# Hybrid encoder step on one core: pool weights folded into the output projection, roots by DRAM, chunk pairs in two column groups, large tiles at multiples of 256 bytes

## The chip, the cores and the metric

The kernel runs on one core of one Trainium2 chip. The metric is the device time of one execution in microseconds (us). A kernel is timed several times and the median counts; beside that, one execution is recorded by the hardware profiler, and its instructions, waits and DMAs make the profile that is read here.

A core has TensorE (PE: matrix products into PSUM), VectorE (DVE), ScalarE (ACT), GpSimd (POOL), and SyncE (SP), which here only issues DMAs.

## The reference, cut to what matters

One layer of a streaming encoder, for a prompt of 2,048 frames and for 32 further frames of a running stream (the sample), with the same weights. All is float32.

```python
h = rmsnorm(x, g_pre_mix)                      # (frames, 1024)
z = h @ w_in                                   # 1024 -> 2560: u | q | f | i | g, 512 each
# mixer A: four groups of 128 channels, windows 2, 4, 8, 16
d = (windowed_sum(u) / count - u)              # per group, trailing window
y_pool = einsum('blgc,gcd->blgd', d, w_pool) * pool_scale
# mixer B: gated linear recurrence, 4 heads x 128, exact, in chunks
o = hgrn(silu(q), (1 - lb) * sigmoid(-f), i, log(lb + (1 - lb) * sigmoid(f)))
y_hg = rmsnorm(o, g_hg_norm) * silu(g)
x = x + rmsnorm(concat(y_pool, y_hg) @ w_out, g_post_mix)
h2 = rmsnorm(x, g_pre_ffn)
x = x + rmsnorm((silu(h2 @ w_gate) * (h2 @ w_up)) @ w_down, g_post_ffn)
```

The outputs are x for prompt and sample, the last 15 rows of u, and the recurrence's final state, for each of the two.

## The kernel before

The prompt is worked in two halves of 1,024 frames, A and B; the 32 sample frames ride along with B. For each half come, in order: the value projection (`vps`), four heads (three projections each into `mmb`, and beside them the recurrence), the four pool groups (one projection each, then window and pool weights), the output projection (`project`, into `ops`), and the gate and up projections (`gate_up`, into `gx`, `gy`, `gz`, `gw`, by a Strassen-like scheme of seven products). After both halves comes the down projection (`down`, into `dx`, `dy`, `dz`).

Each float32 operand of a large product is split into a high and a low part of type float32r, and a product is three matmuls, high x high, high x low and low x high, each of 128 x 128 by 128 x 512 (`mm`, line 179). A half takes 192 of them for the values, 768 for the heads and pool groups, 384 in `project` and 1,848 in `gate_up`; `down` takes 1,848; together 2 x 3,192 + 1,848 = 8,232. The smaller products (recurrence, sums, pool weights, sample) are plain float32; the trace shows each of these as two records.

**What sets the order.** PE's order is the order in which the code emits its instructions. A clock counted in the code (`Pace.t`) adds the cost of every matmul; beside the main stream there are tasks (`Task`: the recurrence of a head, the pool products of a group, the second norm, the statistics of half B), generators that yield a delay. `poll()` runs a task's next step once the clock has passed it, so PE's small products stand among the large ones at chosen distances. `finish()` runs a task to its end on the spot. The orders of the other engines and of the DMA queue of SP are made by a scheduler from what each instruction needs.

**Memory.** Large tiles (`ztile`, `xtile`, lines 90 to 94) come from the pool UP with 39 slots of `TMAX` = 1,056 floats, 4,224 bytes, which is 16.5 x 256: in the built program the slots begin, by turns, at a multiple of 256 bytes and 128 bytes past one. The tiles of 512 floats (`t2`, pool TP, 22 slots of 2,048 bytes) all begin at multiples of 256. Of the operands of large products, `hThi`, `hTlo`, `yhi`, `ylo`, `fhi`, `flo`, `wf`, `dhi`, `dlo` and `whw`, `wlw` lie in UP; `whi`, `wlo` and most of `hst` lie in TP.

**The places that the change touches.**

- Pool groups (`pool_products`, `pool_window`, `pool_mix`, lines 916 to 983): ACT copies a group's projection into `e_t`; DVE makes the trailing window by one to four shifted sums between `sa` and `sb` and a last step that subtracts, emitted in one piece behind the group's projection; later, as a task, PE multiplies by the pool weights `wpool` into `pps` (two float32 products of 128 x 512 for each group and half), and ACT and DVE split the result into `yhi` and `ylo`. In half B the sample's 32 frames go the same way, and two transposes for each group (`nps`) turn the last 15 rows for the outputs.
- `late_constants` (line 153) loads `wpool` and the sample's pool history and transposes the latter (`cps`).
- Roots: the norm of a half multiplies each frame by its reciprocal root. For half B, `later_stats` (line 437) makes the roots as a column for each 128 frames; POOL lays them on a diagonal (`dg`, line 482), and PE multiplies with a matrix of ones to have them along the rows (`rb`, line 457). The sample is normalised by rows and transposed (`stps`, line 369).
- Recurrence (`hgrn`, line 722): 1,024 frames are 8 chunks of 128. Within a chunk, pairwise products are made level by level: `group` (line 736) for blocks of 32 frames, each product 32 columns wide (`gb`, four column groups in turn); then the level of pairs of 32 (line 805, into `gb`, column groups 0 and 2), and the level of 64 (line 811, into `lv`, 64 columns wide, always PSUM rows 0 to 63). ACT copies these last two into `attn` (lines 818 and 819). DVE carries the state from chunk to chunk (`S`, line 873), and the products `ops` read `attn` and `S`. `f_t`, `k_t`, `q_t`, `qa` are a head's gates and keys, `tt` their running products, `kd` the turned keys, `ups` the state's increments, `on` the head's normalised output.

Of the kernel before, what the change touches and what calls it, by code (L numbers as in the profile page):

```python
# [16 lines left out]
P = 128  # L17
D = 1024
# [11 lines left out]
NT = 22  # L30
# [4 lines left out]
TMAX = HALF + NS  # L35
CHUNK = 128
# [41 lines left out]
def body(tc, ins, outs, cst):  # L78
    nc = tc.nc
    ctx = ExitStack()  # L80
    with ctx:
# [7 lines left out]

        def ztile(name, shape=None, dt=F32):  # L90
            return UP.tile(shape or [P, TMAX], dt, tag="u", name=name)

        def xtile(name, shape=None):
            return UP.tile(shape or [P, TMAX], F32R, tag="u", name=name)
# [46 lines left out]
        wpool = CP.tile([P, 4, P], F32, name="wpool")  # L141
        hist = CP.tile([P, 4, 16], F32, name="hist")
        shist = CP.tile([P, 4, 16], F32, name="shist")
# [9 lines left out]
        def late_constants():  # L153
            nc.sync.dma_start(out=wpool, in_=ins["w_pool"][0].rearrange("g c d -> c g d"))
            cachet = ztile("cachet", [HIST, 512])
            nc.sync.dma_start(out=cachet, in_=ins["cache_pool"][0, 0])
            cps = axbank("cps")
            for g in range(4):
                nc.tensor.transpose(cps[:, 16 * g:16 * g + HIST], cachet[:, g * P:(g + 1) * P], ident[0:HIST, 0:HIST])
            nc.vector.tensor_copy(shist[:, :, 0:HIST], cps[:, 0:64].rearrange("p (g t) -> p g t", g=4)[:, :, 0:HIST])  # L160
# [276 lines left out]
        def later_stats(S):  # L437

            st = S.st
            for i in range(NCH):  # L440
                for c in range(2):
                    x = t2("xtl")
                    r0 = S.tok0 + i * P
                    nc.sync.dma_start(out=x, in_=x_p[r0:r0 + P, c * 512:c * 512 + 512])
                    sumsq(x, P, st[:, 2 * i + c:2 * i + c + 1])
                    del x
                yield 20000.0
            ev = st[:, 0:16].rearrange("p (i c) -> p i c", c=2)
# [3 lines left out]
            S.rs = [[st[:, 24 + 4 * tg + i:25 + 4 * tg + i] for i in range(4)] for tg in range(2)]  # L452
# [22 lines left out]
        def front_norm(S, tg):  # L475
            if tg == 0:
                S.hsr = SP.tile([P, KD, NS], F32, tag="hs", name="hsr", bufs=1)
                S.ysr = SP.tile([P, KD, NS], F32, tag="ysr", name="ysr", bufs=1)
            channel_tiles(S, tg)
            S.dg[tg] = t2("dg", [P, 4, P])  # L480
            for i in range(4):
                nc.gpsimd.tensor_scalar(S.dg[tg][:, i], ident, S.rs[tg][i], None, ALU.mult)
            if tg == 1:
                xq = ztile("xts", [NS, D])
                nc.sync.dma_start(out=xq, in_=x_s)
# [3 lines left out]
            if tg == 1:  # L489
                st = new_stat()  # L490
                sumsq(xq, NS, st[0:NS, 0:1])
                nc.vector.tensor_scalar(xq, xq, rstd_of(st, NS), None, ALU.mult)
            yield from scaled_channels(S, tg)
            if tg == 1:
                sample_to_channels(xq, g_pre, S.hsr)


        def front_loads(S):
# [223 lines left out]
        def hgrn(S, H, h):  # L722
# [9 lines left out]
            blks = [(c, j, gb[c // 4][32 * j:32 * j + 32, (c % 4) * 96:(c % 4 + 1) * 96]) for c in range(NCH) for j in range(4)]  # L732
            if B:
                blks.append((NCH, 0, gb[1][32:64, 384:480]))

            def group(goff, src, pick, n=16):
                join()
                for c, j, out in blks:
                    c0 = c * P + 32 * j
                    mm(out[:, goff:goff + n], k_t[:, c0:c0 + 32], pick(src[:, c0:c0 + 32]), True, True, 36.0)  # L740
# [21 lines left out]
            def masked(dst, bank, row0, col0, nch, r):  # L762
                bv = bank[row0:row0 + r, col0:col0 + 96 * nch].rearrange("p (c x) -> p c x", x=96)
                for i in range(NGRP):
                    mk = cons[row0:row0 + r, C_MASK + 16 * i:C_MASK + 16 * i + 16].bitcast(I32).unsqueeze(1).broadcast_to([r, nch, 16])
                    src = bv[:, :, 16 * i:16 * i + 16]
                    if i == 1 or i == 2:
                        src = bv[:, :, 16:48].rearrange("p c (b y) -> p c b y", y=4)[:, :, :, 2 * i - 2:2 * i]
# [32 lines left out]
            for c in range(NCH):  # L801
                o = 384 + (c % 4) * 32
                for j in (0, 2):
                    c0 = c * P + 32 * j
                    mm(gb[c // 4][32 * j:32 * j + 32, o:o + 32], k_t[:, c0:c0 + 32], qa[:, c0 + 32:c0 + 64], True, True, 55.0)
# [4 lines left out]
            for c in range(NCH):  # L810
                mm(lv[0:64, c * 64:c * 64 + 64], k_t[:, c * P:c * P + 64], qa[:, c * P + 64:c * P + 128], True, True, 112.0)
            yield 0.0
            t7 = merge(6, tc_)
            for sb in range(2):
                masked(cmp_[sb], gb[sb], 0, 0, 4, P)
                bv = gb[sb][:, 384:512].rearrange("p (c x) -> p c x", x=32)
                for j in (0, 2):
                    nc.scalar.copy(attn[sb][32 * j:32 * j + 32, :, 32 * j + 32:32 * j + 64], bv[32 * j:32 * j + 32])
                nc.scalar.copy(attn[sb][0:64, :, 64:128], lv[0:64, sb * 256:sb * 256 + 256].rearrange("p (c x) -> p c x", x=64))
                if B and sb == 1:  # L820
                    masked(cmps, gb[1], 32, 384, 1, 32)
# [94 lines left out]
        def pool_products(S, g):  # L916
            e_t = ztile("e_t")
            es = small("es", [P, 48], bufs=2) if S.B else None
            nc.vector.tensor_copy(e_t[:, 0:HIST], hist[:, g, 0:HIST])
            w = take()  # L920
# [7 lines left out]
            S.pools[g] = S.pool = Task(pool_mix(S, g, e_t, es), (9000.0 if S.B else 14000.0) if g > 1 else (7000.0 if S.B else 9000.0), after=S.pool)  # L928
            pool_window(S, g, e_t, es)

        def pool_window(S, g, e_t, es):
            w = WINDOWS[g]

            def window(src, L, bufs, d, first):
# [8 lines left out]
                nc.vector.scalar_tensor_tensor(d[:, 0:L], cur[:, HIST:n], 1.0 / w, src[:, HIST:n], ALU.mult, ALU.subtract)  # L943
# [5 lines left out]
            S.d[g] = sb if w in (2, 8) else sa  # L949
            window(e_t, HALF, (sa, sb), S.d[g], not S.B)  # L950
            if not S.B:
                nc.vector.tensor_copy(hist[:, g, 0:HIST], e_t[:, HALF:HALF + HIST])
            else:
                nc.vector.tensor_copy(es[:, 0:HIST], shist[:, g, 0:HIST])
                s1, s2 = small("es1", [P, 48], bufs=2), small("es2", [P, 48], bufs=2)
                S.ds[g] = s2 if w in (2, 8) else s1
                window(es, NS, (s1, s2), S.ds[g], False)

        def pool_mix(S, g, e_t, es):
            S.y[g] = (ztile("yhi", dt=F32R), ztile("ylo", dt=F32R))  # L960
            d_t = S.d[g]
            for sbk in range(2):
                ps = axbank("pps")
                mm(ps, wpool[:, g, :], d_t[:, sbk * 512:(sbk + 1) * 512], True, True, 858.0)
                hi, lo = S.y[g]
                cols = slice(sbk * 512, (sbk + 1) * 512)
                nc.scalar.activation(hi[:, cols], ps, AF.Copy, scale=p_scale[:, g:g + 1])
                nc.vector.scalar_tensor_tensor(lo[:, cols], ps, p_scale[:, g:g + 1], hi[:, cols].bitcast(F32),
                                               ALU.mult, ALU.subtract)
# [736 lines left out]
```

## Time and profile before

| | |
|---|---|
| Time, median of 3 runs | 2145.66 us (2145.22 to 2146.64) |
| The profiled execution's own time | 2145.8 us |
| Its span, first to last instruction | 2144.0 us |
| PE busy | 2124.1 us (99%), 13,176 matmul records |
| DVE, ACT, POOL busy | 1431.6, 822.0, 281.6 us |
| DMA | 316.19 MB, mean 147 GB/s |
| Granted TensorE clock, mean | 0.998 |

The stages in the profiled execution, roughly: values of half A to 52 us, its heads and pool groups to 292, its output projection to 362, gate and up to 795; half B the same from there to 1,690; the down projection to 2,136; the last rows to 2,144.

How to read the rows that the prediction shows: a group's row gives line, engine, operation, output <- inputs and shape, then busy time and mean duration of one in ns, then idle time ahead of it with what ended it. A matmul's record lasts longer than the distance to the next one, since matmuls overlap in the array; what a matmul costs is read from the distance between starts, or from the time that a stretch takes divided by its matmuls. A timeline row gives the start, the duration in us, and how many records were merged. A window's row gives its length, the busy time with the number of records, the granted clock, the DMA engines' busy share and the rate.

### The profile page before, as it was taken

To read this page: it belongs to the slowest core of one execution; us is meant where nothing else is said; L and a number is where in the kernel's file an instruction comes from. 1 tells how busy PE (TensorE), PEld (TensorE's weight loads), DVE (VectorE), ACT (ScalarE), POOL (GpSimd) and SP (SyncE) were. 2 spreads that over 40 slices of the span, in tenths; PEclk is the share of its full clock that TensorE was granted. 3 is DMA by queue.
4 is the path that set the end of the run, shared out by engine and by line. 5 is a ranking of instruction groups with operands and counts; after the bars stand their busy time and mean duration, and the time that the engine had idled before them with its cause. 6 is when DMAs were issued, how large, how long until landed. Compare 5 with 4: busy or idle time off the path is not lost.

```text
span 2144.0 us, 34134 instructions
## 1 busy us (share of the span) xinstructions
PE 2124.1 (99%) x13176; PEld 1702.8 (79%) x13176; DVE 1431.6 (67%) x2330; ACT 822.0 (38%) x1605; POOL 281.6 (13%) x382
## 2 busy tenths in 40 slices
PE   9999999999999999999999999999999999999998
PEld 8788778888888887788867778888888777877876
DVE  6655665787776778355574697767667756466487
ACT  6434335544444445233323664444444521011032
POOL 1223301100000010122320220000000211110134
PEclk9999999999999999999999999999999999999999
DMA  8121134445545559011004624544445796776778
GB/s 305 50 70 56 35 128 157 128 123 167 157 144 156 148 162 286 27 44 34 25 23 149 189 85 131 156 143 143 144 143 145 234 323 197 224 222 189 223 214 217
DMA packets 388783, 316.19 MB, mean 147 GB/s; under 512 B 16007, under 2 KB 318335, under 8 KB 388622
## 3 DMA queue, kind: packets, MB, share of 16 engines
q1 hardware_dynamic: 386174, 306.11, 46.5%
q0 software_dynamic: 2016, 7.34, 1.8%
q8 instruction: 104, 1.70, 0.3%
q14 instruction: 57, 0.47, 0.1%
q10 hardware_dynamic: 432, 0.57, 0.1%
HBM read 215.60 MB, written 98.37 MB: 146 GB/s over the span
## 4 chain that ended last, share of the span: by engine, by line
PE 82%; DVE 4%; ACT 1%; issue 1%; POOL 1%; DMA 1%; DVEq 0%; POOLq 0%; SPq 0%; ACTq 0%
PE gx L180 21%; PE gy L180 11%; PE dx L180 10%; PE mmb L180 10%; PE ops L180 9%; PE dy L180 5%; PE gz L180 4%; PE dz L180 3%; PE vps L180 2%; PE gw L180 1%; PE gsps L180 1%; PE gb L180 1%; DVE acc L1493 1%; PE ups L180 1%; PE pps L180 1%
## 5 line engine op out<-in xcount | busy, mean ns | idle before, releaser
L180 PE MATMUL gx<-fhi,wf 128*128 128x512 f32 x1376 | 449.1, 395 | 0.0
L180 PEld LDWEIGHTS gx<-fhi,wf 128*128 128x128 f32 x1376 | 258.3, 188 | 61.4 <-issue 2.2
L180 PE MATMUL gx<-flo,wf 128*128 128x512 f32 x688 | 270.0, 392 | 0.0
L180 PE MATMUL gy<-fhi,wf 128*128 128x512 f32 x704 | 233.0, 393 | 0.1
L180 PE MATMUL mmb<-hThi,whi 128*128 128x512 f32 x512 | 217.6, 425 | 0.0
L180 PE MATMUL dx<-dhi,hst 128*128 128x512 f32 x640 | 213.4, 394 | 0.5 <-DVE acc L1493 0.4
L180 PE MATMUL mmb<-hThi,wlo 128*128 128x512 f32 x512 | 201.7, 394 | 0.0
L180 PE MATMUL mmb<-hTlo,whi 128*128 128x512 f32 x512 | 201.5, 394 | 0.0
L1493 DVE TENSOR_TENSOR acc<-dx,acc 128x512 f32<-128x512 f32 x168 | 115.2, 689 | 75.9 <-PE dx L180 75.2
L1217 DVE TENSOR_TENSOR wf<-s,wf 128x512 fp32r<-128x512 f32 x176 | 120.1, 689 | 62.2 <-ACT wf L1212 59.6
L180 PEld LDWEIGHTS gy<-fhi,wf 128*128 128x128 f32 x704 | 132.2, 188 | 31.2 <-DVE c L1315 0.5
L180 PEld LDWEIGHTS gx<-flo,wf 128*128 128x128 f32 x688 | 129.4, 188 | 28.3
L1212 ACT CAST wf<-s 128x512 fp32r<-128x512 f32 x176 | 108.3, 621 | 101.0 <-PE gy L180 30.3
L180 PEld LDWEIGHTS dx<-dhi,hst 128*128 128x128 f32 x640 | 120.1, 188 | 32.2 <-issue 3.4
L180 PE MATMUL gy<-flo,wf 128*128 128x512 f32 x352 | 138.2, 393 | 0.0
L180 PE MATMUL dx<-dlo,hst 128*128 128x512 f32 x320 | 125.5, 392 | 0.0
L1217 DVE TENSOR_TENSOR wf<-wraw,wf 128x512 fp32r<-128x512 f32 x132 | 89.8, 688 | 44.2 <-ACT wf L1212 44.1
L180 PEld LDWEIGHTS mmb<-hThi,whi 128*128 128x128 f32 x512 | 96.6, 189 | 24.4 <-issue 5.4
L180 PEld LDWEIGHTS mmb<-hThi,wlo 128*128 128x128 f32 x512 | 96.4, 188 | 22.3
L180 PE MATMUL dy<-dhi,hst 128*128 128x512 f32 x320 | 112.9, 393 | 1.0 <-DVE acc L1493 1.0
L1212 ACT CAST wf<-wraw 128x512 fp32r<-128x512 f32 x132 | 80.9, 621 | 83.5 <-PE gx L180 38.3
L180 PEld LDWEIGHTS mmb<-hTlo,whi 128*128 128x128 f32 x512 | 96.8, 189 | 18.7 <-issue 2.4
(332 smaller groups left out, 4093.2 us busy)
## 6 DMA issues: line engine op xcount, KB each, us to landing
hst<-hdFalse SPq DMA_DIRECT2D x140, 256.0 KB, 3.0
hst<-hdTrue SPq DMA_DIRECT2D x140, 256.0 KB, 3.1
wraw<-in_w_gate_dram SPq DMA_DIRECT2D x50, 512.0 KB, 4.2
wraw<-in_w_up_dram SPq DMA_DIRECT2D x50, 512.0 KB, 4.1
hdFalse<-hhi SPq DMA_DIRECT2D x77, 256.0 KB, 2.3
hdFalse<-hlo SPq DMA_DIRECT2D x77, 256.0 KB, 2.4
hdTrue<-hhi SPq DMA_DIRECT2D x77, 256.0 KB, 2.6
hdTrue<-hlo SPq DMA_DIRECT2D x77, 256.0 KB, 2.6
```

The source lines that it names most:

```text
L180: nc.tensor.matmul(out, l, r, start=start, stop=stop, skip_group_check=more)
L1212: nc.scalar.copy(wf[:, 0], getattr(M, src) if isinstance(src, str) else src)
L1217: nc.vector.tensor_tensor(wf[:, 1], getattr(M, src) if isinstance(src, str) else src, wf[:, 0].bitcast(F32), ALU.subtract)
L1493: nc.vector.tensor_tensor(dst, ps, dst, ALU.add)
```

## The change

1. **Pool weights.** `wpool` times the rows of `w_out` that it meets is the same for every frame. A task in half A (`mixed_weights`) makes the 512 x 1,024 product on PE (eight float32 products of 128 x 512 into `wmp`, with the scales put on the transposed weights by ACT), copies it out by ACT (`wmo`) and writes it to DRAM (`mixed`); `project` loads those rows from there instead of `w_out`. The pool products `pps` go; the window's result is split directly. The window is now itself a task, one shifted sum for each step.
2. **Last rows.** The 15 last rows of each group are gathered by POOL in one tile and turned by one transpose at the end; the sample's pool history comes already by channels in an input.
3. **Roots.** `later_stats` also makes the sample's roots and writes all roots to DRAM; they are loaded back, repeated over the 128 partitions (`rb`, `rbs`). `dg`, the products with ones and the transposes of the sample are gone in half B; the sample comes by channels.
4. **Chunk pairs.** In the two upper levels odd chunks go to other PSUM rows than even ones, so that consecutive products stand in four column groups (`gb`) and in two (`lv`). ACT copies twice as many pieces of half the size.
5. **Tiles.** Slots of UP are `SLOT` = 1,088 floats, 4,352 bytes, 17 x 256, and in the built program all 39 begin at multiples of 256. TP has 21 slots instead of 22.

```diff
-NT = 22
+NT = 21
+SLOT = HALF + 64
         def ztile(name, shape=None, dt=F32):
-            return UP.tile(shape or [P, TMAX], dt, tag="u", name=name)
+            return UP.tile(shape or [P, SLOT], dt, tag="u", name=name)
...
+        roots = DP.tile([1, TMAX], F32, name="roots")
+        mixed = DP.tile([4 * P, D], F32, name="mixed")
+        def mixed_weights():
+            wt = t2("wpt", [P, 4, P])
+            nc.sync.dma_start(out=wt, in_=ins["w_pool_t"].rearrange("g d c -> d g c"))
+            rows = {}
+            todo = [(g, dh) for g in (2, 3, 0, 1) for dh in range(2)]
+            def load(g, dh):
+                rows[g, dh] = t2("wmr")
+                nc.sync.dma_start(out=rows[g, dh], in_=w_out[g * P:(g + 1) * P, dh * 512:dh * 512 + 512])
+            load(*todo[0])
+            yield 6000.0
             for g in range(4):
+                nc.scalar.activation(wt[:, g], wt[:, g], AF.Copy, scale=p_scale[:, g:g + 1])
+            for n, (g, dh) in enumerate(todo):
+                if n + 1 < len(todo):
+                    load(*todo[n + 1])
+                ps = axbank("wmp")
+                mm(ps, wt[:, g], rows.pop((g, dh)), True, True, 858.0)
+                out = t2("wmo")
+                nc.scalar.copy(out, ps)
+                nc.sync.dma_start(out=mixed[g * P:(g + 1) * P, dh * 512:dh * 512 + 512], in_=out)
+                del out, ps
+                yield 4000.0
...
+            nc.sync.dma_start(out=roots[0, 0:HALF].rearrange("(i p) -> p i", p=P), in_=st[:, 24:32])
+            nc.sync.dma_start(out=roots[0, HALF:TMAX].rearrange("(p i) -> p i", i=1), in_=st[0:NS, 35:36])
         def scaled_channels(S, tg):
-            rb = axbank("rb")
-            for i in range(4):
-                mm(rb[:, i * P:(i + 1) * P], ones, S.dg[tg][:, i], True, True, 112.0)
+            if S.B:
+                rb = S.rb[tg]
+            else:
+                rb = axbank("rb")
+                for i in range(4):
+                    mm(rb[:, i * P:(i + 1) * P], ones, S.dg[tg][:, i], True, True, 112.0)
...
+            S.rb[tg] = t2("rb")
+            nc.sync.dma_start(out=S.rb[tg], in_=roots[0:1, tg * 512:tg * 512 + 512].broadcast_to([P, 512]))
             channel_tiles(S, tg)
-            S.dg[tg] = t2("dg", [P, 4, P])
-            for i in range(4):
-                nc.gpsimd.tensor_scalar(S.dg[tg][:, i], ident, S.rs[tg][i], None, ALU.mult)
...
+                nc.sync.dma_start(out=S.hsr, in_=ins["x_sample_channels"].rearrange("(k p) t -> p k t", p=P))
...
-                    want(lambda ki=ki, dh=dh: raw_rows2(w_out, KORDER[ki], dh * 512))
+                    want(lambda ki=ki, dh=dh: raw_rows2(mixed if KORDER[ki] < 4 else w_out, KORDER[ki], dh * 512))
...
             for c in range(NCH):
-                o = 384 + (c % 4) * 32
+                o = 384 + c % 4 // 2 * 32
                 for j in (0, 2):
-                    c0 = c * P + 32 * j
-                    mm(gb[c // 4][32 * j:32 * j + 32, o:o + 32], k_t[:, c0:c0 + 32], qa[:, c0 + 32:c0 + 64], True, True, 55.0)
+                    c0, q = c * P + 32 * j, 32 * (j + c % 2)
+                    mm(gb[c // 4][q:q + 32, o:o + 32], k_t[:, c0:c0 + 32], qa[:, c0 + 32:c0 + 64], True, True, 55.0)
...
             for c in range(NCH):
-                mm(lv[0:64, c * 64:c * 64 + 64], k_t[:, c * P:c * P + 64], qa[:, c * P + 64:c * P + 128], True, True, 112.0)
+                q, o = c % 2 * 64, c // 2 * 64
+                mm(lv[q:q + 64, o:o + 64], k_t[:, c * P:c * P + 64], qa[:, c * P + 64:c * P + 128], True, True, 112.0)
...
-            S.pools[g] = S.pool = Task(pool_mix(S, g, e_t, es), (9000.0 if S.B else 14000.0) if g > 1 else (7000.0 if S.B else 9000.0), after=S.pool)
-            pool_window(S, g, e_t, es)
+            S.pools[g] = S.pool = Task(pool_window(S, g, e_t, es), 1500.0, after=S.pool)
...
                     nc.vector.tensor_tensor(nxt[:, a:n], cur[:, a:n], cur[:, a - lev:n - lev], ALU.add)
                     cur, lev, i = nxt, 2 * lev, i + 1
+                    yield 1300.0 if L > NS else 0.0
...
-            for sbk in range(2):
-                ps = axbank("pps")
-                mm(ps, wpool[:, g, :], d_t[:, sbk * 512:(sbk + 1) * 512], True, True, 858.0)
+            put_y(S, g, slice(0, HALF), d)
...
-            late_constants()
...
+                    Task(mixed_weights(), 4000.0)
```

How the rows move on three engines, at the places that the prediction speaks of. First PE, at the end of the last head of half A: before, the last state products `ops` are followed by the pool products.

```order
L180 MATMUL ops_2940<-vb,attn_742 128x128
L180 MATMUL ops_2940<-S,qa 128x128
L180 MATMUL pps<-sa,wpool 128x512
L180 MATMUL mmb<-hThi_328,whi 128x512
L180 MATMUL mmb<-hTlo_329,whi 128x512
L180 MATMUL mmb<-hThi_328,wlo 128x512
L180 MATMUL pps<-sa,wpool 128x512
```

In the changed program the same place:

```order
L200 MATMUL ops_3019<-vb,attn_769 128x128
L200 MATMUL ops_3019<-S,qa 128x128
L200 MATMUL mmb<-hThi_326,whi 128x512
L200 MATMUL mmb<-hTlo_327,whi 128x512
L200 MATMUL mmb<-hThi_326,wlo 128x512
```

Sixteen products `pps` among the pool groups and `project` are gone from PE's order. From the first head of half A, one of the eight products that make the mixed weights, and what follows it:

```order
L200 MATMUL wmp<-wmr,wpt 128x512
L200 MATMUL mmb<-hThi_318,whi 128x512
L200 MATMUL mmb<-hTlo_319,whi 128x512
L200 MATMUL mmb<-hThi_318,wlo 128x512
L200 MATMUL mmb<-hThi_320,whi 128x512
```

The eight `wmp` stand 14 to 17 rows apart among the first head's projections.

Second DVE, at the start of the last head's recurrence in half B, before (`tt<-f_t` is the first running product of the gates, `sa` and `sb` the window of the widest pool group):

```order
L914 TENSOR_TENSOR ysr<-yps,g_t 128x32
L941 TENSOR_TENSOR es_10266<-es_10265 128x32
L943 SCALAR_TENSOR_TENSOR es_10265<-es_10266,es 128x32
L941 TENSOR_TENSOR sa<-e_t 128x1038
L941 TENSOR_TENSOR sb<-sa 128x1036
L919 COPY e_t<-hist 128x15
L941 TENSOR_TENSOR sa<-sb 128x1032
L941 TENSOR_TENSOR sb<-sa 128x1024
L943 SCALAR_TENSOR_TENSOR sa<-sb,e_t 128x1024
L759 TENSOR_TENSOR tt<-f_t 128x528
```

and in the changed program:

```order
L760 TENSOR_TENSOR qa<-q_t,f_t 128x1056
L750 TENSOR_TENSOR ylo<-yr,yhi 128x512
L791 TENSOR_TENSOR qa<-qa,f_t 128x528
L958 COPY e_t<-hist 128x15
L946 SCALAR_TENSOR_TENSOR S_10223<-S_10201,tt,ups 128x128
L792 TENSOR_TENSOR tt<-f_t 128x528
```

The window stands behind the running product now, not ahead of it.

Third DVE again, at the end of the same head, where the state goes from chunk to chunk; before:

```order
L941 TENSOR_TENSOR sa<-e_t 128x1038
L941 TENSOR_TENSOR sb<-sa 128x1036
L943 SCALAR_TENSOR_TENSOR sa<-sb,e_t 128x1024
L919 COPY e_t<-hist 128x15
L873 SCALAR_TENSOR_TENSOR S<-state_91,tt,ups 128x128
L873 SCALAR_TENSOR_TENSOR S<-S,tt,ups 128x128 x6
```

and in the changed program:

```order
L910 SCALAR_TENSOR_TENSOR S<-state_89,tt,ups 128x128
L910 SCALAR_TENSOR_TENSOR S<-S,tt,ups 128x128 x3
L981 TENSOR_TENSOR sa<-e_t 128x1038
L910 SCALAR_TENSOR_TENSOR S<-S,tt,ups 128x128
L981 TENSOR_TENSOR sb<-sa 128x1036
L910 SCALAR_TENSOR_TENSOR S<-S,tt,ups 128x128
L984 SCALAR_TENSOR_TENSOR sa<-sb,e_t 128x1024
L910 SCALAR_TENSOR_TENSOR S<-S,tt,ups 128x128
```

The first four states come ahead of the window of a pool group, and the other states stand between its steps.

More of the change, by code (lines that the diff above doesn't have):

```diff
@@ L959, in pool_mix @@
[L959 to L970 removed]
+                nc.gpsimd.tensor_copy(S.tail[:, 0, g], e_t[:, HALF:HALF + HIST])
@@ L971, in pool_mix @@
+                nc.gpsimd.tensor_copy(S.tail[:, 1, g], es[:, NS:NS + HIST])
+            yield from window(e_t, HALF, (sa, sb), d, not S.B)
+            yield 1300.0
+            S.y[g] = (ztile("yhi", dt=F32R), ztile("ylo", dt=F32R))
+            put_y(S, g, slice(0, HALF), d)
             if S.B:
                 yield 0.0
-                ps = axbank("pps")
-                mm(ps[:, 0:NS], wpool[:, g, :], S.ds[g][:, 0:NS], True, True, 218.0)
-                nc.vector.tensor_scalar(S.ysr[:, g, :], ps[:, 0:NS], p_scale[:, g:g + 1], None, ALU.mult)
@@ L976, in pool_mix @@
[L976 to L977 removed]
+                yield from window(es, NS, [small(n, [P, 48], bufs=1) for n in ("es1", "es2")], S.ysr[:, g, :], False)
+                if g == 0:
                     ps = axbank("nps")
[L979 removed]
+                    nc.tensor.transpose(ps[0:8 * HIST, 0:P], S.tail.rearrange("p s g t -> p (s g t)"), ident)
                     tick(107)
[L981 to L983 removed]
+                    npl = small("S0", [8 * HIST, P], bufs=2)
+                    nc.vector.tensor_copy(npl, ps[0:8 * HIST, 0:P])
+                    for i in range(8):
+                        out = outs[4 if i // 4 else 2]
+                        nc.sync.dma_start(out=out[0, 0, :, i % 4 * P:(i % 4 + 1) * P], in_=npl[i * HIST:(i + 1) * HIST])
```

101 lines of the change are left out of this document (49 added, 52 removed).

## The prediction

> **What bounds the kernel now.** I read the page's busy times first, then the waits of PE, then windows by stage, then the timeline of PE.
>
> ```profile
> PE 2124.1 (99%) x13176; PEld 1702.8 (79%) x13176; DVE 1431.6 (67%) x2330; ACT 822.0 (38%) x1605; POOL 281.6 (13%) x382
> PE gb L180 <- ACT f_t L789: 2.5, 1, 2.5
> PE gb L180 <- POOL k_t L757: 1.8, 1, 1.8
> PE gb L180 <- DVE qa L758: 1.5, 1, 1.5
> 420.00:720.00 300.00, 300.00 (x1301) 1.00 0.49 144
> 790.00:845.00 55.00, 55.00 (x253) 44.90 (x252) 51.22 (x76) 32.95 (x53) 4.07 (x6) 1.00 0.81 254
> ```
>
> PE is busy for 2124.1 of 2144.0 us and waits little: the three longest waits come to 5.8 us. Everything else lies beside it. The fifth row is a window on PE in a gate-and-up stage: always busy, at full clock (1.00), with 1,301 matmuls in 300 us, 230.6 ns for each. So there are two ways to a shorter time: fewer PE instructions, or a shorter distance between them. There are 8,232 large matmuls, and one nanosecond on each is 8.2 us. The last row, with busy times of PE, weight load, DVE, ACT and POOL in turn, shows the one stage where another engine is near full: DVE 51.22 of 55 us.
>
> **Begin addresses.** The distance is not the same everywhere, so I laid the built program's addresses beside the timeline. The rows are PE's near the end of the down projection (the first three), and in the output projections of half B (the next two) and half A (the last two); start and duration in us lead each row:
>
> ```profile
> 2116.44 0.39 PE L180 MATMUL dx<-dlo,hst 128*128 128x512 f32 x1
> ...
> 2120.29 0.39 PE L180 MATMUL dx<-dhi,hst 128*128 128x512 f32 x1
> ...
> 2124.44 0.39 PE L180 MATMUL dx<-dhi,hst 128*128 128x512 f32 x1
> ...
> 1153.97 0.39 PE L180 MATMUL ops<-whi,yhi 128*128 128x512 f32 x1
> ...
> 1156.70 0.40 PE L180 MATMUL ops<-whi,yhi 128*128 128x512 f32 x1
> ...
> 324.97 0.40 PE L180 MATMUL ops<-whi,yhi 128*128 128x512 f32 x1
> ...
> 327.78 0.39 PE L180 MATMUL ops<-whi,yhi 128*128 128x512 f32 x1
> ```
>
> From 2116.44, 17 matmuls take 3.85 us, 226.5 ns each: there every `dhi`, `dlo` and `hst` begins at a multiple of 256. The next 18 take 4.15 us, 230.6 each: there some operands begin 128 bytes past one. In `ops` 12 matmuls take 2.73 us (227.5) where all operands begin at multiples, and 2.81 us (234.2) in the other half, where `yhi` begins 128 past and the rest does not. In the program before, 2,652 of the 8,232 large matmuls have both operands at multiples of 256, mostly in short runs; in the changed program all have. I take 227.0, the middle of 226.5 and 227.5: 3.6 ns on 8,232, **-29.6**. It applies to all 8,232, since the window's 230.6 is a mean over both kinds. Bounds: 0, if something else sets the pitch, and 4.1 x 8,232 = -33.8 at 226.5.
>
> The Trainium skill ("SBUF — State Buffer", Who interferes with whom) says that "PE and ACT never wait on anyone", and names no penalty for a begin address. By that rule this term would be 0 and the sum 2126.3; the two pairs of rows above speak against it as far as they go.
>
> **Pool weights.** The rows are PE's at a pool product and the two matmuls behind it.
>
> ```profile
> 262.54 1.02 PE L180 MATMUL pps<-sa,wpool 128*128 128x512 f32 x2
> 263.00 0.79 PE L180 MATMUL mmb<-hThi,whi 128*128 128x512 f32 x1
> 263.63 0.39 PE L180 MATMUL mmb<-hTlo,whi 128*128 128x512 f32 x1
> ```
>
> From the product's start to the first plain matmul behind its follower is 1.09 us; less that follower's own 0.23, a product costs 0.86. Sixteen go (-13.8), eight `wmp` of the same shape come (+6.9): **-6.9**. The eight stand beside the first head's projections, far ahead of `project`. Their row loads are 256 KB and each is asked for one 4 us step ahead; the writes wait on ACT's copies, and weight prefetches stand behind them in SP's queue, but a product every 16 matmuls (3.7 us) asks for little. I cost that at nothing.
>
> **Small products that go.** Groups of PE by shape, then two rows of its timeline:
>
> ```profile
> L180 PE MATMUL rb<-dg,ones 128*128 128x128 f32 x32 | 4.2, 274 | 0.0
> L979 PE MATMUL nps<-cons,es 128*15 128x128 f32 x4 | 1.1, 275 | 0.0
> L979 PE MATMUL nps<-cons,e_t 128*15 128x128 f32 x4 | 1.1, 274 | 0.4 <-DVE on L838 0.4
> L369 PE MATMUL stps<-cons,xts 32*128 32x32 f32 x8 | 0.7, 225 | 0.0
> L159 PE MATMUL cps<-cons,cachet 15*128 15x15 f32 x4 | 0.4, 213 | 0.0
> L180 PE MATMUL pps<-es,wpool 128*128 128x32 f32 x8 | 1.3, 246 | 0.0
> 261.19 0.39 PE L180 MATMUL ops<-va,attn 128*128 128x128 f32 x2
> 261.42 0.39 PE L180 MATMUL ops<-S,qa 128*128 128x128 f32 x2
> ```
>
> A float32 product of 128 columns costs 0.23, the distance of the last two rows. Of the 32 records of `rb` 16 belong to half B, 8 products: **-1.8**. The five rows behind `rb` are 4.6 us busy; one transpose comes back, and records overlap, so I take **-3.0** (2.0 to 4.3). The sample's loads by channels come at the start, ahead of the first weights in SP's queue; PE's first need of those is far behind.
>
> **Chunk pairs.** Bursts of the recurrence, before:
>
> ```profile
> 85.91 0.76 PE L180 MATMUL gb<-f_t,k_t 128*32 128x32 f32 x64
> 98.56 0.70 PE L180 MATMUL gb<-qa,k_t 128*32 128x32 f32 x32
> 103.55 1.15 PE L180 MATMUL lv<-qa,k_t 128*64 128x64 f32 x16
> 246.35 0.45 PE L180 MATMUL lv<-qa,k_t 128*64 128x64 f32 x4
> 256.17 0.39 PE L180 MATMUL ops<-S,qa 128*128 128x128 f32 x2
> L818 ACT COPY attn<-gb 32x128 f32<-32x128 f32 x32 | 8.2, 255 | 19.9 <-DVE cmp L781 19.7
> L819 ACT COPY attn<-lv 64x256 f32<-64x256 f32 x16 | 5.4, 368 | 2.8 <-PE lv L180 2.7
> ```
>
> Sixty-four records in four column groups take 0.76 us; 32 in two groups take 0.70. In four groups these 32 should take 0.38: -0.32 for each of eight heads, **-2.6**. The 64-wide burst stands in one group and takes 1.15; in two, about half, -0.5 each, **-4.0**. No row shows two groups of 64, so both bounds reach to 0. ACT makes twice the copies; at most the same 255 and 368 ns again, 1.8 us a head, against 9.8 us from `lv` to the products that read `attn` (fourth and fifth row): hidden.
>
> **The wait that goes.** The end of the last head's gates in half B, on DVE, ACT and PE, and PE's window there:
>
> ```profile
> 1068.47 1.24 DVE L941 TENSOR_TENSOR sa<-e_t 128x1038 f32<-128x1038 f32 x1
> ...
> 1074.80 1.23 DVE L943 SCALAR_TENSOR_TENSOR sa<-sb,e_t 128x1024 f32<-128x1024 f32 x1
> 1076.06 0.71 DVE L759 TENSOR_TENSOR tt<-f_t 128x528 f32<-128x528 f32 x1
> 1076.86 0.67 ACT L789 COPY f_t<-q_t 128x528 f32<-128x528 f32 x1 [1.81 <-DVE tt L759]
> 1078.23 1.18 PE L180 MATMUL gb<-f_t,k_t 128*32 128x32 f32 x66 [2.54 <-ACT f_t L789]
> 1077.50:1081.50 4.00, 3.27 (x71) 0.57 0.02 4
> ```
>
> DVE works five window steps from 1068.47 to 1076.03; only then comes `tt`, then ACT's `f_t`, and PE has waited 2.54 us. The clock granted behind it is 0.57, so in 4.00 us some 1.7 are lost: together 4.2. In the changed order `tt` stands ahead of the window: **-4.2**, bounds 0 and -5. What is late next is `k_t` and `qa` (1.8 and 1.5, above), which I leave as they are.
>
> **Waits that come.** Window steps now stand between states. Before, in half A's last head, on DVE:
>
> ```profile
> 254.48 0.28 DVE L871 COPY S<-ups 128x128 f32<-128x128 f32 x1
> ```
>
> The states came right behind the window, 1.7 us ahead of the first product that reads one (256.17). Now a step of 1.24 us stands behind each of the last states in half B, while PE takes one state product each 0.45 us (two rows of 0.23). PE's second group of chunks must then wait about 1 to 1.5 us there, and in half A a `ylo`, which itself waits for ACT, stands between two states. Behind a wait on DVE are queued the window's next step and the weight splits. I take **+3**, bounds 0 and +8 (two such places with a wait and a clock loss as above, 4.2 each).
>
> **Sum.** -6.9 - 1.8 - 3.0 - 2.6 - 4.0 is -18.3 for fewer or denser instructions; -29.6, -4.2 and +3 make **-49.1**. The profiled execution's own time is 2145.8 (span 2144.0 and 1.8 around it), 0.1 from the median of the runs: 2096.7, so **2097**.
>
> **Rivals.**
>
> *Begin addresses make nothing.* The short distances could come from something else that differs in these stretches: fewer transfers, or which tile is stationary. Against it: the products of the down projection are alike in all but the addresses, and lie 4 us apart. Then -18.3 - 4.2 + 3 is left: **2126.3**. Chance 0.09.
>
> *New waits eat a part.* The window as a task puts 1.24 us steps ahead of whatever DVE owes PE, in each head with a pool group beside it, not only in the last. At the price above, 4.2 each, four more such places are 17 us: **2114**. For it: 51.22 of 55 us of DVE at the output projection, where `ylo` and the splits of weights compete. Against it: there and in the heads PE waited for almost nothing. Chance 0.10, of which 0.01 that they eat nearly all and the time stays.
>
> *Slower: one begin for all is the bad one.* The addresses matter, but by the meeting of the two operands rather than by the remainder: the aligned stretches were fast since neighbouring matmuls came from differently placed slots, and 39 slots at one remainder put both reads on the same side each time. Price: the slow row's 234.2 for all, 3.6 over 230.6, is +29.6 on 2126.3, **2156**. It decides from a distance of 233.0 ns on, where 2.4 x 8,232 eats the 19.5 that the rest gives. Against it: the 17 matmuls at 226.5 had all operands at one remainder. Chance 0.03.
>
> **How the numbers follow.** The forecast has 0.78, the rivals 0.09, 0.10 and 0.03. Main case with the best bounds: -4.2 more for the pitch, -1.7 for the structure and the wait, -3 without new waits, **2088**. At the worst of its bounds the column groups give nothing (+6.6), new waits 8 (+5), and the pitch is 228 (+8); all three together would be 2117. The range ends at **2116** and takes in the second rival; outside lie the first, the third and the tails. A difference under 0.2% (4.3 us) can't be told from no change. Faster by more: main, first rival and the second but for 0.01, 0.96; same 0.01; slower 0.03.
>
> **What would show it.** In the changed profile a window inside gate and up should hold about 1,321 matmuls in 300 us, not 1,301; 1,301 would be the first rival, under 1,290 the third. PE busy should be about 2075 (2124.1 less 18.3, 29.6 and the 1.7 of the clock). `pps` and `dg` are gone, `wmp` x16 records at about 600 ns; `lv` bursts last about 0.6, the level below 0.4. The wait of `gb` on `f_t` is off PE's list; an entry of `ops` on `S` or `ylo` of 1 to 2 us is the new wait, and entries over 2.5 us at several heads the second rival. I am wrong if the windows stay at 230 ns, or if waits of PE sum to over 20 us.

## The result, and the profile after

The changed kernel takes 2113.06 us (median of 4 runs, 2111.08 to 2116.41) against 2145.73 before: a ratio of 0.9851, 95% interval 0.9836 to 0.9865. The forecast was 2097, with a range of 2088 to 2116. Direction and range hold, but 16 us of the gain that the forecast counted on are missing. Its runs lie 5.3 us apart; in the later series runs of the kernel before lie up to 5.4 apart too, so nothing is read from that. The profiled execution took 2111.08 us.

The page's busy times after, then the window in gate and up, then waits of PE, then two bursts in half A's first head, by the timeline:

```profile
PE 2080.8 (99%) x13117; PEld 1689.4 (80%) x13117; DVE 1421.3 (67%) x2302; ACT 832.1 (39%) x1659; POOL 284.8 (14%) x387
```

```profile
420.00:720.00 300.00, 300.00 (x1324) 1.00 0.50 146
```

```profile
PE gb L200 <- POOL k_t L790: 5.0, 1, 5.0
PE mmb L200 <- issue: 4.2, 1, 4.2
...
PE gb L200 <- ACT f_t L821: 0.4, 2, 0.2
PE ops L200 <- DVE S L910: 0.3, 1, 0.3
```

```profile
102.46 0.46 PE L200 MATMUL gb<-qa,k_t 128*32 128x32 f32 x32
...
107.18 0.69 PE L200 MATMUL lv<-qa,k_t 128*64 128x64 f32 x16
```

Much is as forecast. The window holds 1,324 matmuls in 300 us, 226.6 ns each, where 1,301 stood. The wait of `gb` on `f_t` is down from 2.5 to 0.4, the feared wait of `ops` on `S` is 0.3, and the bursts are down from 0.70 to 0.46 and from 1.15 to 0.69. But the two longest waits are new or longer: 5.0 us on POOL's `k_t` (1.8 before), and 4.2 us that the profile can only call "issue": PE had its data and still did not go on. The matmuls' starts, laid beside those of before one by one, show where it happened: in the last head of half A, within 12 us.

The waits in that stretch, all engines, after; a row names the waiting engine and tile, what released it, the sum, the count and the longest:

```profile
ACT junk L312 <- DMA xsl<-in_x_sample_dram: 11.1, 2, 10.5
POOL k_t L790 <- issue: 7.9, 1, 7.9
DVE qa L791 <- PE gb L200: 7.3, 2, 6.7
POOL k_t L790 <- remote: 7.1, 1, 7.1
...
PE gb L200 <- POOL k_t L790: 5.0, 1, 5.0
...
PE mmb L200 <- issue: 4.2, 1, 4.2
DVE qa L791 <- remote: 4.2, 1, 4.2
```

"Remote" is a release by a semaphore (a counter by which one engine tells another that it is done) for which the view finds no setter. Three waits have no visible reason: POOL's 7.1 us, DVE's 4.2 and PE's 4.2. POOL's 7.9 is called "issue" too, but POOL goes on at 251.40, right behind PE's `gb` that ends at 251.25, so it is PE's lateness handed on. The first two end together: DVE goes on at 238.97, POOL at 239.07, and the trace has PE's semaphore, which both wait for, rise at 238.94. By its record, whose end is modelled, the `gb` that sets it ends at 233.45. So by the trace POOL and DVE waited for a late signal of PE. What was going on beside them is in the DMA queue of SP, by the timeline, and in the DMA view of 226 to 262 us (issues with KB and us to landing):

```profile
229.23 0.38 SPq L481 DMA_DIRECT2D roots<-st_b  x1
229.66 0.58 SPq L251 DMA_DIRECT2D wraw<-in_w_in_dram  x1
230.33 0.54 SPq L258 DMA_DIRECT2D wrow<-in_w_out_dram  x1
230.96 0.88 SPq L470 DMA_DIRECT2D xsl<-in_x_sample_dram  x2
```

```profile
q8 instruction: 3, 0.05, 1.1%
...
wraw<-in_w_in_dram SPq DMA_DIRECT2D x1, 512.0 KB, 14.6
wrow<-in_w_out_dram SPq DMA_DIRECT2D x1, 512.0 KB, 15.5
xsl<-in_x_sample_dram SPq DMA_DIRECT2D x2, 64.0 KB, 15.4
roots<-st_b SPq DMA_DIRECT2D x1, 4.0 KB
```

And the same view of before, 222 to 262 us:

```profile
q8 instruction: 3, 0.05, 0.5%
...
wrow<-in_w_out_dram SPq DMA_DIRECT2D x2, 512.0 KB, 3.4
```

At 229.23 the changed kernel writes half B's roots to DRAM. They lie as a column for each 128 frames, so the 4 KB go as 1,024 single floats. Loads issued behind it land after 15 us, where 512 KB took 3.4 before. Instructions come by DMA too (queue q8): 104 packets over the kernel, against 26,234 records of PE and its weight loads, one for each 250 or so, so they look like PE's. The three in these 36 us took 1.1% of 16 engines, 2.1 us each, against 0.5% over 40 us, 1.1 each, before. But the mean misleads. The same view for 226 to 250 us, then for 250 to 262:

```profile
q8 instruction: 2, 0.03, 0.6%
```

```profile
q8 instruction: 1, 0.02, 2.0%
```

Two fetches took some 1.1 us each, as before, and the long one, 3.9 us, starts at 257.61, behind all the stops. What differs is when they come: before, fetches start at 232.71 and 238.92, here none between 223.76 and 245.06. The one at 245.06 ends at 246.20, and PE goes on at 247.59. All this gives a theory for what is missing.

### The profile page after: what moved, and what is told of

Same layout as the page of the kernel before. It is cut to its first block, busy times and chain, and to the rows that moved or that the text cites. A ratio compares the mean times of both kernels' runs of the same rounds, so it can differ in the third digit from the quotient of the medians.

```text
span 2109.3 us, 34101 instructions
## 1 busy us (share of the span) xinstructions
PE 2080.8 (99%) x13117; PEld 1689.4 (80%) x13117; DVE 1421.3 (67%) x2302; ACT 832.1 (39%) x1659; POOL 284.8 (14%) x387
## 4 chain that ended last, share of the span: by engine, by line
PE 77%; DVE 7%; DMA 1%; issue 1%; ACT 1%; POOL 1%; SPq 0%; DVEq 0%; POOLq 0%; ACTq 0%
PE gx L200 20%; PE gy L200 10%; PE mmb L200 10%; PE dx L200 10%; PE ops L200 8%; PE dy L200 5%; PE gz L200 4%; PE dz L200 2%; DVE acc L1521 1%; PE gw L200 1%; PE gsps L200 1%; PE vps L200 1%; PE gb L200 1%; PE ups L200 1%; DMA rb<-roots 1%
## 5 line engine op out<-in xcount | busy, mean ns | idle before, releaser
L200 PE MATMUL gx<-fhi,wf 128*128 128x512 f32 x1376 | 444.2, 391 | 0.0
L200 PEld LDWEIGHTS gx<-flo,wf 128*128 128x128 f32 x688 | 129.2, 188 | 26.1
```

The source lines that it names most:

```text
L200: nc.tensor.matmul(out, l, r, start=start, stop=stop, skip_group_check=more)
```

## The theory, a rival, and the experiments

**Theory.** The begin addresses, the fewer products and the column groups gave about what was forecast; the scattered write of the roots takes most of the difference back. It holds up the DMA engines for some 10 us, the loads and instruction fetches behind it come late, POOL, DVE and PE run dry in turn, and PE runs at a reduced clock behind the waits. (For POOL and DVE the late semaphore above already speaks against this last link.) **Rival.** POOL and DVE are late there by the work that was moved (window steps, copies), the write is harmless, and the begin addresses gave less than the window shows, or nothing.

**1. Only the large slots.** The kernel before, with one slot less of each kind of tile to make room.

```diff
-NU = 39
-NT = 22
+NU = 38
+NT = 21
-            return UP.tile(shape or [P, TMAX], dt, tag="u", name=name)
+            return UP.tile(shape or [P, SLOT], dt, tag="u", name=name)
```

> The kernel before with the large slots at 4,352 bytes and nothing else but the room for it (38 slots instead of 39, 21 small ones instead of 22). Theory (begin addresses set the distance): 8,232 matmuls come 3.2 to 3.6 ns sooner, 26 to 29 us, so 2117 to 2120 us, and the window 420 to 720 us holds about 1,323 matmuls. Rival (addresses make nothing, the gain of the change is all from fewer products): 2145 to 2147 us and 1,301 matmuls.

Measured: 2125.46 us, ratio 0.9905 (0.9891 to 0.9918), 20 us faster. Its window, then two of PE's waits:

```profile
420.00:720.00 300.00, 300.00 (x1324) 1.00 0.52 150
```

```profile
PE dx L180 <- DVE acc L1493: 2.0, 4, 0.7
...
PE pps L180 <- DVE sa L943: 1.8, 1, 1.8
```

The window is that of the changed kernel to the matmul. The gain fell short of the expected 26 to 29 us. PE's busy time fell by 25.7 us (2124.1 to 2098.4), but its idle time rose from 19.9 to 26.1: some waits grew (two are shown; before, `dx` on DVE was 0.4 us). That the missing slots made them grow is likely, but wasn't tried apart. And the gain isn't even: between the 960th and the 3,072nd large matmul, in the output projection and gate and up, the starts draw 8.7 us ahead of those of before, 4.1 ns each; between the 192nd and the 768th, in the heads, only 1.0 us, 1.7 ns each.

**2. The slots back.** The changed kernel, with each engine's instructions in the same order.

```diff
-SLOT = HALF + 64
+SLOT = TMAX
```

> The changed kernel with the large slots back at 4,224 bytes; every engine's order stays. Theory (begin addresses): 26 to 29 us longer than the changed kernel's 2113, so 2139 to 2142 us. Rival (addresses make nothing): 2111 to 2116 us, as the changed kernel.

Measured: 2137.0 us, ratio to before 0.9957 (0.9943 to 0.997), 24 us slower than the changed kernel. The window:

```profile
420.00:720.00 300.00, 300.00 (x1304) 1.00 0.49 142
```

Back at 230 ns. The rival's "addresses make nothing" is out. The size is 24 us by the medians, somewhat under the 26 expected; the two profiled executions lie 26.5 apart, so it is known to some 2 us. Here too the heads gain less: 1.2 ns for each matmul between the 192nd and the 768th, 3.5 between the 960th and the 3,072nd.

**3. The roots as rows.** One transpose on PE turns the eight columns; the write is eight rows of 512 bytes. It also comes at 356 us instead of 229, since the transpose stands there in PE's order.

```diff
-            nc.sync.dma_start(out=roots[0, 0:HALF].rearrange("(i p) -> p i", p=P), in_=st[:, 24:32])
+            yield 3000.0
+            ps = axbank("rps")
+            nc.tensor.transpose(ps[0:NCH, 0:P], st[:, 24:32], ident)
...
+            rt = t2("rt", [NCH, P])
+            nc.scalar.copy(rt, ps[0:NCH, 0:P])
+            nc.sync.dma_start(out=roots[0, 0:HALF].rearrange("(i p) -> i p", p=P), in_=rt)
```

> The changed kernel with half B's 1,024 roots turned by one transpose and written to DRAM as eight rows of 512 bytes, not as 1,024 single floats. Theory (the scattered write holds up the DMA engines and with them the loads and the engines' instructions, which makes PE's waits of 5.0 and 4.2 us near 240 us and the half clock behind): both waits go, 2100 to 2104 us, and the runs lie within 1 us. Rival (POOL and DVE are late there by the window's steps and the copies, not by the write): the waits stay, 2111 to 2116 us.

Measured: 2098.9 us (2097.7 to 2099.26), ratio 0.978 (0.9767 to 0.9794), 14 us faster than the changed kernel and a little better than expected. PE's longest waits, and the window 225 to 265 us, first here, then in the changed kernel:

```profile
PE gb L200 <- DVE qa L798: 1.9, 5, 0.7
PE dy L200 <- DVE acc L1528: 1.1, 1, 1.1
```

```profile
225.00:265.00 40.00, 39.46 (x484) 1.00 0.10 28
```

```profile
225.00:265.00 40.00, 30.59 (x410) 0.87 0.16 31
```

Both waits are gone. PE is busy for 39.46 of 40 us at full clock, not for 30.59 at 0.87. The runs lie within 1.6 us, not the 1 that was expected. Since form and place of the write changed together, the next experiments part them.

**4. The scattered write alone.** Added to the kernel before, at its place, into a tile that nobody reads.

```diff
             S.rs = [[st[:, 24 + 4 * tg + i:25 + 4 * tg + i] for i in range(4)] for tg in range(2)]
+            nc.sync.dma_start(out=roots[0, 0:HALF].rearrange("(i p) -> p i", p=P), in_=st[:, 24:32])
```

> The kernel before with the same write of 1,024 single floats to DRAM added at the same place, read by nobody. Theory (the scattered write): loads issued behind it land after 10 us or more, not 3.4, some engines stop for want of instructions, and the time is 5 to 12 us longer, 2151 to 2158 us. Rival (late POOL and DVE): 2145 to 2147 us.

Measured: 2152.27 us, ratio 1.0029 (1.0018 to 1.004), 6.7 us slower. Its first wait of PE, PE's timeline there, and the load behind the write:

```profile
PE gb L182 <- issue: 4.7, 1, 4.7
```

```profile
235.06 0.49 PE L182 MATMUL gb<-qa,k_t 128*32 128x16 f32 x34
240.28 0.92 PE L182 MATMUL gb<-qa,k_t 128*32 128x16 f32 x30 [4.74 <-issue]
```

```profile
wrow<-in_w_out_dram SPq DMA_DIRECT2D x1, 512.0 KB, 12.6
```

Nothing else of the change is in this kernel, and the wait on "issue" is there. So the write makes PE stop. How it does so is open. Here PE stops after 34 of the 64 records of one `gb` and goes on at 240.28, before the next fetch of instructions starts (242.37), so no late fetch ended this stop; and DVE and POOL have no wait on "issue" or "remote" of more than 2 us. In the changed kernel the stop that ends at 247.59 does follow a late fetch, by 1.4 us, and so it does in experiment 2, where that fetch ends at 247.41 and PE goes on at 248.85. The changed kernel has a second wait, of 5.0 us on POOL's late `k_t`, that this one lacks; 14 there against 6.7 here goes with that.

**5. The same bytes in 128 pieces,** from the same place, still read by nobody.

```diff
-...out=roots[0, 0:HALF].rearrange("(i p) -> p i", p=P), in_=st[:, 24:32])
+...out=roots[0, 0:HALF].rearrange("(p i) -> p i", p=P), in_=st[:, 24:32])
```

> The kernel before with the same 4 KB written at the same place as in scatter_only, but as 128 runs of 32 bytes. Theory (the cost goes with the number of single writes): under 1.5 us, 2145 to 2147 us, loads behind land after 3 to 5 us. Rival (any write of pieces this small to DRAM there holds the engines up): as scatter_only, 2150 to 2153 us.

Measured: 2145.64 us, ratio 1.0001 (0.9993 to 1.001). The issues in 222 to 262 us:

```profile
wrow<-in_w_out_dram SPq DMA_DIRECT2D x2, 512.0 KB, 3.5
roots<-st_b SPq DMA_DIRECT2D x1, 4.0 KB, 1.4
```

Same bytes, queue and moment, and no cost. The place alone isn't it. Whether the number of pieces counts or the size of each, these two runs don't part: 128 pieces in 1.4 us are 11 ns for each as well.

**6. The scattered write later.** The changed kernel, with the write at 346 us, near where experiment 3 has its rows (356), by way of a copy on ACT.

```diff
-            nc.sync.dma_start(out=roots[0, 0:HALF].rearrange("(i p) -> p i", p=P), in_=st[:, 24:32])
+            yield 3000.0
+            rt = t2("rt", [P, NCH])
+            nc.scalar.copy(rt, st[:, 24:32])
+            nc.sync.dma_start(out=roots[0, 0:HALF].rearrange("(i p) -> p i", p=P), in_=rt)
```

> The changed kernel with the 1,024 single floats still written one by one, but some 125 us later, in the output projection of half A, as the rows are in roots_rows. Theory (the write holds up loads and instructions wherever it stands): 2103 to 2112 us, with a wait on issue near 360 us. Rival (what counts is the place: only beside the last head's short products does PE run dry): 2098 to 2100 us.

Measured: 2107.84 us, ratio 0.9823 (0.981 to 0.9837), 8.9 us over experiment 3. The write's own issue, and three waits between 340 and 380 us:

```profile
roots<-rt SPq DMA_DIRECT2D x1, 4.0 KB, 11.8
```

```profile
DVE wlo L244 <- ACT whi L243: 7.3, 1, 7.3
ACT whi L243 <- DMA wrow<-in_w_out_dram: 7.1, 1, 7.1
...
PE ops L200 <- DVE h2raw L346: 4.6, 1, 4.6
```

The 1,024 floats land after 11.8 us, 11.5 ns each. The time came as expected, but not by the expected wait: there is no "issue" here. The load behind the write is late for ACT, ACT for DVE, and DVE for PE. Both places have a price, and it reaches PE by different ways; but it is 8.9 us here against 14 at the first place, so the rival is right in part, and the place counts as well.

**7. Two scattered writes.** As experiment 4, with a second one into another tile.

```diff
+            nc.sync.dma_start(out=more[0, 0:HALF].rearrange("(i p) -> p i", p=P), in_=st[:, 24:32])
```

> The kernel before with two such writes of 1,024 single floats, one behind the other, read by nobody. Theory (each single write takes its turn, some 11 ns): they land after 22 to 26 us, PE waits for instructions about twice as long, 10 to 20 us over the kernel before, 2156 to 2166 us. Rival (a fixed price for a scattered transfer, shared by two in a row): as scatter_only, 2150 to 2154 us.

Measured: 2156.22 us, ratio 1.0047 (1.0031 to 1.0064), 10.7 us over before. PE's first wait, and the load issued behind the two writes:

```profile
PE gb L182 <- issue: 6.4, 7, 3.2
```

```profile
wrow<-in_w_out_dram SPq DMA_DIRECT2D x1, 512.0 KB, 21.1
```

The load lands 8.5 us later than behind one write (21.1 against 12.6), about as the theory says. The time grows less than in proportion, at the lower edge of the expected range: PE now stops seven times, 3.2 us at most. How PE's loss grows with the number of floats isn't settled by this.

**8. The other way.** Experiment 4 with a load of 1,024 single floats, into columns that are no longer needed.

```diff
-            nc.sync.dma_start(out=roots[0, 0:HALF].rearrange("(i p) -> p i", p=P), in_=st[:, 24:32])
+            nc.sync.dma_start(out=st[:, 0:8], in_=ins["g_post_mix"][0, :].rearrange("(i p) -> p i", p=P))
```

> The kernel before with a load of 1,024 single floats from DRAM at the place of the write in scatter_only, into columns that nobody reads any more. Theory in its narrow form (it is the writing of 4 bytes to DRAM that is slow): 2145 to 2147 us, landing within 4 us. Rival (the number of packets counts, whichever way they go): 5 to 8 us over the kernel before, 2150 to 2154 us.

Measured: 2145.76 us, ratio 1.0001 (0.9992 to 1.0011). The issues:

```profile
wrow<-in_w_out_dram SPq DMA_DIRECT2D x2, 512.0 KB, 3.6
st_b<-in_g_post_mix_dram SPq DMA_DIRECT2D x1, 4.0 KB, 2.2
```

Queue q1 has 387,214 packets in this kernel and in that of experiment 4, against 386,174 before. The same number of packets read from DRAM lands in 2.2 us and costs nothing, though it was issued 2.5 us earlier, since it waits for no roots. It is writing single floats to DRAM that is slow.

**9. The column groups back,** in the kernel of experiment 3.

```diff
-                o = 384 + c % 4 // 2 * 32
+                o = 384 + c % 4 * 32
-                    c0, q = c * P + 32 * j, 32 * (j + c % 2)
+                    c0, q = c * P + 32 * j, 32 * j
-                q, o = c % 2 * 64, c // 2 * 64
+                q, o = 0, c * 64
...
```

> The kernel of roots_rows (2098.9 us) with the two upper levels in the column groups of before, and ACT's copies as before. Theory (the column groups are worth the forecast's 6.6 us): 2103 to 2106 us, the burst of 16 records lv at 1.15 us again. Rival (they are hidden or eaten by ACT's added copies): 2098 to 2100 us.

Measured: 2105.87 us, ratio 0.9813 (0.98 to 0.9827), 7.0 us over experiment 3. The bursts, first here, then in experiment 3:

```profile
102.10 0.70 PE L200 MATMUL gb<-qa,k_t 128*32 128x32 f32 x32
...
107.03 1.15 PE L200 MATMUL lv<-qa,k_t 128*64 128x64 f32 x16
```

```profile
102.01 0.46 PE L200 MATMUL gb<-qa,k_t 128*32 128x32 f32 x32
...
106.71 0.69 PE L200 MATMUL lv<-qa,k_t 128*64 128x64 f32 x16
```

A head gains 0.24 and 0.46 by these rows, eight heads 5.6; the forecast had 6.6, and the medians give 7.0, with this kernel's runs 2.9 us apart (2104.32 to 2107.22), so that all three fit. ACT's added copies, which the edit takes back as well, eat nothing that shows.

**10. The window in one piece,** in the kernel of experiment 3.

```diff
             S.pools[g] = S.pool = Task(pool_window(S, g, e_t, es), 1500.0, after=S.pool)
+            S.pool.finish()
```

> The kernel of roots_rows with each pool group's window emitted in one piece behind its projection, so that it stands ahead of the running products tt on DVE again. Theory (the wait of gb on f_t and the half clock behind it, 4.2 us, went because the window became a task): the wait of 2.5 us or more is back, 2102 to 2105 us. Rival (the window's place decides nothing in this kernel): 2098 to 2100 us.

Measured: 2109.71 us, ratio 0.9832 (0.9818 to 0.9845), 10.8 us over experiment 3 and more than expected. PE's waits, and DVE ahead of the first of them:

```profile
PE gb L200 <- ACT f_t L828: 5.4, 3, 5.1
PE ops L200 <- DVE S L917: 1.5, 2, 1.2
```

```profile
1054.23 1.23 DVE L992 SCALAR_TENSOR_TENSOR sa<-sb,e_t 128x1024 f32<-128x1024 f32 x1
...
1056.57 1.23 DVE L757 TENSOR_TENSOR ylo<-sa,yhi 128x1024 fp32r<-128x1024 f32 x1 [0.91 <-ACT yhi L756]
1057.71 0.17 DVE L965 COPY e_t<-hist 128x15 f32<-128x15 f32 x1
1057.79 0.70 DVE L799 TENSOR_TENSOR tt<-f_t 128x528 f32<-128x528 f32 x1
```

With the pool weights folded away, `ylo` follows the window at once, waits for ACT and stands ahead of `tt` as well; so the wait is 5.1, not the 2.5 of before. The edit finishes the whole task on the spot, splits and all, while the kernel before split later; the window in one piece with a later split wasn't tried. So 10.8 us is the price of both in one piece.

## Why the prediction came out as it did

- **What bounds the kernel.** Right: the time follows PE's distance and PE's waits in every experiment.
- **Begin addresses, -29.6.** The mechanism is right, the size too large: 24 to 26 us in the changed kernel (experiment 2), 20 alone (experiment 1). The step that failed was applying 3.6 ns to all 8,232. The streams from the output projection on give 4.1 (experiment 1) and 3.5 (experiment 2), but the heads, where small products break the stream, 1.7 and 1.2. Why short runs gain less wasn't tried.
- **The Trainium skill's sentence** that PE never waits on anyone ("SBUF — State Buffer", Who interferes with whom) was read in the forecast as 0 for this term, 2126 in all. The sentence is about engines that hold up each other at the memory's ports; it says nothing on where an operand begins, so the reading went too far. The traces show a price: 1,304 against 1,324 matmuls in the same window, with nothing but the slot size between them. What in the chip makes the difference isn't shown.
- **Roots.** This step failed by leaving out a cost. The forecast took off 1.8 us for `rb`'s products and priced nothing for the write that replaces them, though the changed code shows a column written as single floats. The write costs 14 us where it stands (experiment 3 against the changed kernel); experiments 4, 5 and 8 tie that to single floats written to DRAM. This is the larger part of the missing 16 us. That the time still lies in the range is in part luck: its upper end, 2116, was built from column groups that give nothing, new waits of 8 us and a distance of 228 ns, and none of these came about. (At the lower end its -1.7 for structure and wait is -2.1 by its own bounds, which makes 2087 of 2088.)
- **Column groups, -6.6.** Right: 5.6 by the bursts, 7.0 by the medians.
- **The wait on `f_t`, -4.2.** It went, as forecast: 0.4 is left of 2.5, and the clock in 1054 to 1070 us, around the last head's first `gb`, is 1.00. The 4.2 itself wasn't measured apart; experiment 10's 10.8 has the splits in it too.
- **Pool weights and small products, -11.7, and new waits, +3.** Not tried apart. What they come to together can be worked out: from before to experiment 3 it is 2145.7 - 2098.9 = 46.8 faster; less 24 for the addresses, 7.0 for the groups and 4.2 for the wait, 11.6 is left, uncertain by some 2 us as the 24 is, and with a 4.2 that is the forecast's own. That is near the products' 11.7 with no new waits, where the forecast had 8.7. PE's idle time in experiment 3 says the same: 18.0 us (2095.7 - 2077.7) against 19.9 before, and `ops` on `S` is 0.3 by the rows above.
- **The rivals.** The second named the right size, 2114 against 2113, and the wrong cause: with the window's steps where they are, the waits go when the write does (experiment 3), and they stand at one place, not at four. That the median fell on the rival's number is chance.

The forecast's own sign for being wrong, "over 20 us of waits", was just about reached: the profile's list of PE's waits adds up to 19.9 us, and the idle time of PE rose from 19.9 (2144.0 - 2124.1) to 28.5 us (2109.3 - 2080.8), start and end included. Of the 8.6 more, 7.4 are the two waits of 5.0 and 4.2 less the 1.8 of before.

The fastest kernel here is that of experiment 3, 2098.9 us: the change with its roots written as rows.

## What to carry to other kernels

Price each DMA that replaces arithmetic by its number of pieces and its direction, not by its bytes; a column laid on partitions should be turned before it is written to DRAM. When several engines stop at once for "issue" or "remote", look for what the DMA engines were doing just ahead. And where PE streams large matmuls, look up at what addresses their tiles begin: 128 bytes of padding for each slot were worth 24 us here.

## What the runs showed of the hardware

- 1,024 single floats written to DRAM landed after 11.8 us, and loads behind them in the queue after 12.6 to 15.5 us instead of 3.4. The same 4 KB in 128 pieces landed after 1.4 us, and 1,024 single floats read from DRAM after 2.2.
- Beside such a write PE stopped for 4.2 to 4.8 us with nothing to wait for (experiments 2 and 4 and the changed kernel). In the changed kernel and experiment 2 a fetch of PE's instructions ended 1.4 us before PE went on; in experiment 4 none did. A semaphore of PE rose 5.5 us behind the modelled end of the `gb` that sets it, and POOL and DVE waited for it. How the write does this isn't shown.
- Large matmuls whose operands begin at multiples of 256 bytes came every 226.6 ns in the long streams (1,324 in 300 us); with some operands 128 bytes past one, every 230.1 to 230.6 (1,304 and 1,301).
- The same 32 records of 32 columns took 0.70 us in two column groups and 0.46 in four, 16 records of 64 columns 1.15 us in one and 0.69 in two.
